# One low half in four by an adding DMA: a split float32 weight stream in a GLA and retention trunk

## The chip, the cores and the metric

The kernel runs on one core of a Trainium2 chip. The metric is device time in microseconds (us) from the start to the end of the program. Engines are named as in the profile: PE is TensorE (matrix products), PEld its weight loads, DVE is VectorE, ACT is ScalarE, POOL is GpSimd, SP is SyncE, which here only issues DMAs. "SPq" and "POOLq" are the DMA issues on the queues of SP and POOL.

## The reference

Two layers on 256 tokens of width 2048, in float32: a gated linear attention layer (GLA, 4 heads) and a retention layer (8 heads). Each normalises its input, projects it by a wide matrix to q, k, v and a gate, runs the attention in chunks of 64, normalises per head, multiplies by SiLU of the gate and projects back:

```python
proj = h @ w_in
q, k, v, gate = jnp.split(proj, [...], axis=-1)
...                                    # attention in chunks, per head
return (o * jax.nn.silu(gate)) @ w_out
```

The four weight matrices are almost all of the data that the program reads, and the products with them almost all of its arithmetic.

## The kernel before

The weights are laid out by the host as 60 groups; a group is 2048 x 512, that is 16 blocks of 128 x 512. A group is worked off in eight **sub-tiles** of two blocks each (`SUB = 2`), so there are 480 sub-tiles, in one fixed order from the first layer to the last. Each group is one product: q and k of a head (`group_w`, where the weights are the stationary operand), or v, the gate or a quarter of the output projection (`group_x`, where the activations are stationary).

TensorE multiplies here in a shorter float format (`F32R`). To keep float32 accuracy every operand is split in two: `hi` is the operand rounded to that format, and `lo` is the rest, operand minus `hi`. A product is then three matmuls, x_hi by w_hi, x_hi by w_lo, x_lo by w_hi (`mm3`, lines 184 to 186; lines 216 to 220 in `group_w`). The splits of the activations (`xhl`, `ogt`) are kept; those of the weights are made on the way:

- SP loads raw weights in tiles of 1 MB, two sub-tiles each, into three buffers (`emit_raw`, line 118), two tiles ahead (`DMA_LOOK`).
- ACT writes `hi` of a sub-tile as a rounding copy (line 151), DVE writes `lo` as raw minus hi (line 152). Each is 128 partitions by 1024 elements. There are three `hi` and three `lo` buffers.
- PE runs the 12 (`group_x`) or 16 (`group_w`) matmuls of the sub-tile.

`next_weights` is called once for each sub-tile, before its matmuls, and first emits all splits up to `LOOK = 2` ahead. So sub-tile i+2 takes the buffer that sub-tile i-1 used, and ACT can begin on it when PE has finished with i-1. The last group's eight splits go into memory that is free by then (`split_tiles`).

All other work (evacuating PSUM at the end of a group, the decays and scores of GLA, the rotary products, normalisation, transposes) is emitted between the sub-tiles in small steps (`side`, `advance`). The order on each engine is not that of the program text: a scheduler with its own timeline orders the instructions of each engine before the program is built, and each engine then runs its own list in order. POOL has little to do: eight loads each of `dm`, `gg` and `gb` and four of `fn` for the retention heads and the final norm, one of the positions, and 56 small additions in the GLA scores (line 568).

Of the kernel before, what the change touches and what calls it, by code (L numbers as in the profile page):

```python
# [10 lines left out]
F32 = mybir.dt.float32  # L11
F32R = mybir.dt.float32r
BF16 = mybir.dt.bfloat16
I32 = mybir.dt.int32
AF = mybir.ActivationFunctionType
ALU = mybir.AluOpType

P = 128
# [4 lines left out]
GW = 512  # L23
SUB = 2
NSUB = NKT // SUB
CHUNK = 4
LOOK = 2
DMA_LOOK = 2
GLA_H, RET_H, HK = 4, 8, 256
LEVELS = [1, 2, 4, 8, 16, 32, 64]  # L30
SCALE = 1.0 / 16.0
# [24 lines left out]
def kernel(  # L56
# [17 lines left out]
    nc = tc.nc  # L74
    pool = lambda name, bufs, **kw: ctx.enter_context(tc.tile_pool(name=name, bufs=bufs, **kw))
    one = pool("one", 1)
    raw_p = pool("raw", 3)
    hi_p = pool("hi", 3)
    lo_p = pool("lo", 3)
    v_p = pool("v", 2)  # L80
    o_p = pool("o", 2)
    sg_p = pool("sg", 2)
# [21 lines left out]
    last0 = (n_groups - 1) * NSUB  # L104

    def emit_raw(parts=1):
        c = emitted["raw"]
        if c >= n_groups * raws_per_group:
            return
        t = raw_p.tile([P, CHUNK, GW], F32, tag="raw", name=f"raw{c}")  # L110
        g, j = divmod(c, raws_per_group)
        src = w_all[g, :, j * CHUNK * GW : (j + 1) * CHUNK * GW].rearrange("p (k n) -> p k n", n=GW)
        step = CHUNK // parts
        raws[c] = t
        emitted["raw"] += 1

        def load(k):
            nc.sync.dma_start(t[:, k * step : (k + 1) * step, :], src[:, k * step : (k + 1) * step, :])

        if parts > 1:  # L120
            return load
        load(0)

    def split_tiles(i):
        if i < last0:
            hi = hi_p.tile([P, SUB, GW], F32R, tag="hi", name=f"hi{i}")
            lo = lo_p.tile([P, SUB, GW], F32R, tag="lo", name=f"lo{i}")
            return hi, lo
        j = i - last0
        hi = xhl[:, j * SUB : (j + 1) * SUB].rearrange("p k a t -> p k (a t)")  # L130
        if j < 4:
            if j % 2 == 0:
                tails.append(v_p.tile([P, 2, SUB, GW], F32R, tag="v", name=f"tail{j}"))
            return hi, tails[-1][:, j % 2]
        return hi, t4_p.tile([P, SUB, GW], F32R, tag="t4", name=f"tail{j}")
# [3 lines left out]
    def emit_split(pieces=1):  # L139
        i = emitted["sub"]  # L140
        if i >= n_groups * NSUB:
            return
        c, j = divmod(i, per_raw)
        while emitted["raw"] <= min(c + DMA_LOOK, n_groups * raws_per_group - 1):
            emit_raw()
        src = raws[c][:, j * SUB : (j + 1) * SUB, :]
        hi, lo = split_tiles(i)
        step = SUB // pieces
        for k in range(pieces):
            sl = slice(k * step, (k + 1) * step)  # L150
            nc.scalar.activation(hi[:, sl], src[:, sl], AF.Copy)  # L151
            nc.vector.tensor_tensor(lo[:, sl], src[:, sl], hi[:, sl].bitcast(F32), ALU.subtract)  # L152
        splits[i] = (hi, lo)
        if j == per_raw - 1:
            del raws[c]
        emitted["sub"] += 1
# [17 lines left out]
    def next_weights():  # L174
        i = state["sub"]
        while emitted["sub"] <= min(i + LOOK, n_groups * NSUB - 1):
            emit_split()
        state["sub"] += 1
        return splits.pop(i)
# [131 lines left out]
    emit_raw()  # L311
    make_xhl(0)
    emit_split(2)
    make_xhl(1)
    wa1 = t4_p.tile([P, NKT, 48], F32R, tag="lc", name="wa1", bufs=1)
# [676 lines left out]
```

## Time and profile before

| | |
|---|---|
| median of two runs | 1444.03 us (1443.39 to 1444.67) |
| span of the profiled execution, first to last instruction | 1441.2 us |
| PE busy | 1429.9 us |
| DVE, ACT, POOL busy | 910.3, 690.0, 44.1 us |
| granted TensorE clock | 0.999 |
| read from HBM | 263.49 MB |

The profile gives one execution. Its own time is its span, 1441.2 us; the median of the runs is 2.8 us above that, since a run's time also holds what lies before the first and after the last instruction. A group of instructions is shown as line, engine, operation, output tile, input tiles, shapes and count, then the busy time in us and the mean duration in ns, then the idle time of that engine just before these instructions and what ended it. In the timeline the columns are start, duration, engine, line, and in brackets how long the engine had been idle and who released it. Matmuls are pipelined, so that their durations overlap; their spacing is read from the starts.

### The profile page before, as it was taken

The numbers are of one execution on the slowest core, as the hardware profiler recorded it, in microseconds if no ns is written. First come the engines' busy times: TensorE is split into PE (matmuls) and PEld (weight loads), VectorE is DVE, ScalarE is ACT, GpSimd is POOL, SyncE is SP. The second block draws the span as 40 slices with busy tenths as digits, with TensorE's granted clock in tenths as the row PEclk, the third lists the DMA queues.
The fourth block names the chain that finished last, engine by engine and source line by source line (L and its number), as shares of the span: only waits on it lengthen the run. The fifth ranks groups of instructions, "written<-read, shape, count | busy, mean of one in ns | idle before, by whom it ended". The sixth has DMA issues, their size and how long they took to land.

```text
span 1441.2 us, 17504 instructions
## 1 busy us (share of the span) xinstructions
PE 1429.9 (99%) x6800; PEld 1181.0 (82%) x6800; DVE 910.3 (63%) x1430; ACT 690.0 (48%) x889; POOL 44.1 (3%) x98
## 2 busy tenths in 40 slices
PE   9999999999999999999999999999999999999997
PEld 6788888888888888888888888888888888888887
DVE  7595785545845764655666666664546666666654
ACT  4665654533554645454444444444344444444443
POOL 0010010000000010000000000000000000000000
PEclk9999999999999999999999999999999999999999
DMA  8643554555545555555555555555555555554562
GB/s 288 250 170 135 206 178 154 189 184 182 177 170 177 183 183 176 175 175 180 192 187 191 188 183 195 178 193 178 197 180 181 194 179 199 176 204 170 202 207 93
DMA packets 40499, 266.72 MB, mean 185 GB/s; under 512 B 4880, under 2 KB 5392, under 8 KB 9696
## 3 DMA queue, kind: packets, MB, share of 16 engines
q1 hardware_dynamic: 37536, 257.57, 51.2%
q0 software_dynamic: 2160, 6.95, 1.4%
q8 instruction: 53, 0.87, 0.2%
q10 hardware_dynamic: 720, 1.09, 0.2%
q14 instruction: 30, 0.25, 0.0%
HBM read 263.49 MB, written 2.10 MB: 184 GB/s over the span
## 4 chain that ended last, share of the span: by engine, by line
PE 99%; DMA 0%; SPq 0%; DVE 0%; ACT 0%; issue 0%
PE rqk_ps L219 8%; PE gv_ps L184 4%; PE gg_ps L185 4%; PE rv_ps L186 4%; PE gg_ps L186 4%; PE rv_ps L185 4%; PE rg_ps L185 4%; PE gv_ps L186 4%; PE rg_ps L186 4%; PE gv_ps L185 4%; PE rv_ps L184 4%; PE gg_ps L184 4%; PE rg_ps L184 4%; PE rqk_ps L220 4%; PE gqk_ps L219 4%; PE ra_ps L186 2%
## 5 line engine op out<-in xcount | busy, mean ns | idle before, releaser
L152 DVE TENSOR_TENSOR lo<-raw,hi 128x1024 fp32r<-128x1024 f32 (+1 forms) x473 | 577.6, 1223 | 439.9 <-ACT hi L151 421.5
L151 ACT ACTIVATE hi<-raw 128x1024 fp32r<-128x1024 f32 (+1 forms) x473 | 499.4, 1057 | 640.0 <-PE rg_ps L186 77.9
L219 PE MATMUL rqk_ps<-xhl,hi 128*128 128x512 f32 x480 | 165.9, 394 | 0.0
L220 PE MATMUL rqk_ps<-xhl,lo 128*128 128x256 f32 x480 | 127.2, 281 | 0.0
L219 PEld LDWEIGHTS rqk_ps<-xhl,hi 128*128 128x128 f32 x480 | 88.9, 188 | 16.1
L185 PE MATMUL gg_ps<-lo,xhl 128*128 128x512 f32 x256 | 102.1, 399 | 0.0
L185 PE MATMUL rv_ps<-lo,xhl 128*128 128x512 f32 x256 | 102.0, 399 | 0.0
L185 PE MATMUL gv_ps<-lo,xhl 128*128 128x512 f32 x256 | 102.0, 398 | 0.0
L186 PE MATMUL gv_ps<-hi,xhl 128*128 128x512 f32 x256 | 101.9, 398 | 0.0
L186 PE MATMUL gg_ps<-hi,xhl 128*128 128x512 f32 x256 | 101.7, 397 | 0.0
L186 PE MATMUL rv_ps<-hi,xhl 128*128 128x512 f32 x256 | 101.4, 396 | 0.0
L186 PE MATMUL rg_ps<-hi,xhl 128*128 128x512 f32 x256 | 101.3, 396 | 0.0
L185 PE MATMUL rg_ps<-lo,xhl 128*128 128x512 f32 x256 | 101.3, 396 | 0.0
L184 PE MATMUL gv_ps<-hi,xhl 128*128 128x512 f32 x256 | 94.7, 397 | 0.0
L184 PE MATMUL rv_ps<-hi,xhl 128*128 128x512 f32 x256 | 93.5, 396 | 0.0
L184 PE MATMUL rg_ps<-hi,xhl 128*128 128x512 f32 x256 | 93.5, 396 | 0.0
L184 PE MATMUL gg_ps<-hi,xhl 128*128 128x512 f32 x256 | 93.3, 397 | 0.0
L220 PEld LDWEIGHTS rqk_ps<-xhl,lo 128*128 128x128 f32 x480 | 89.2, 189 | 3.5
L219 PE MATMUL gqk_ps<-xhl,hi 128*128 128x512 f32 x240 | 80.0, 402 | 0.6 <-ACT hi L151 0.6
L220 PE MATMUL gqk_ps<-xhl,lo 128*128 128x256 f32 x240 | 57.6, 282 | 0.8 <-DVE lo L152 0.8
L186 PEld LDWEIGHTS rg_ps<-hi,xhl 128*128 128x128 f32 x256 | 48.1, 188 | 11.6
L185 PEld LDWEIGHTS rg_ps<-lo,xhl 128*128 128x128 f32 x256 | 48.1, 188 | 11.5
(265 smaller groups left out, 2395.2 us busy)
## 6 DMA issues: line engine op xcount, KB each, us to landing
raw<-in_w_all SPq DMA_DIRECT2D x238, 1024.0 KB, 4.8
resid<-in_x_n SPq DMA_DIRECT2D x2, 1024.0 KB, 7.8
gg<-in_gn_g POOLq DMA_DIRECT2D x8, 256.0 KB, 3.6
gb<-in_gn_b POOLq DMA_DIRECT2D x8, 256.0 KB, 4.5
dm<-in_dmat POOLq DMA_DIRECT2D x8, 192.0 KB, 2.6
raw<-in_w_all SPq DMA_DIRECT2D x4, 256.0 KB, 4.4
raw<-in_w_all SPq DMA_DIRECT2D x2, 512.0 KB, 7.3
xt<-in_x_t SPq DMA_DIRECT2D x2, 512.0 KB, 9.1
```

The lines of the kernel that those rows point to most:

```text
L151: nc.scalar.activation(hi[:, sl], src[:, sl], AF.Copy)
L152: nc.vector.tensor_tensor(lo[:, sl], src[:, sl], hi[:, sl].bitcast(F32), ALU.subtract)
L184: mm(ps, xh, hi[:, q, :], start=kt == 0, stop=False)
L185: mm(ps, xh, lo[:, q, :], start=False, stop=False)
L186: mm(ps, xl, hi[:, q, :], start=False, stop=kt == NKT - 1)
L219: mm(ps[c], wh, rhs[:, kt, :, :], start=kt == 0, stop=False)
L220: mm(ps[c][:, 0, :], wl, rhs[:, kt, 0, :], start=False, stop=False)
```

## The change

For the sub-tiles 11, 15, 19, ... 471 (from number 8 on, and outside the last group, each fourth one) `lo` is made in another way. ACT writes `hi` as before, then writes minus `hi` into a tile of a new pool with two buffers; then a DMA issued from POOL's queue reads the raw weights of the sub-tile a second time from HBM, 512 KB, and adds them onto that tile in SBUF. DVE has no part in these sub-tiles. In the other sub-tiles nothing changes.

Beside it `LOOK` goes from 2 to 3 and the `hi` pool from three to four buffers. The memory that the program sets aside for the descriptors of POOL's DMAs is set to 4096 bytes.

```diff
-LOOK = 2
+LOOK = 3
+ADDED = 4
+FIRST_ADDED = 8
...
-    hi_p = pool("hi", 3)
+    hi_p = pool("hi", 4)
     lo_p = pool("lo", 3)
+    add_p = pool("add", 2)
...
             hi = hi_p.tile([P, SUB, GW], F32R, tag="hi", name=f"hi{i}")
-            lo = lo_p.tile([P, SUB, GW], F32R, tag="lo", name=f"lo{i}")
+            if FIRST_ADDED <= i and i % ADDED == ADDED - 1:
+                lo = add_p.tile([P, SUB, GW], F32R, tag="add", name=f"added{i}")
+            else:
+                lo = lo_p.tile([P, SUB, GW], F32R, tag="lo", name=f"lo{i}")
...
+        if FIRST_ADDED <= i < last0 and i % ADDED == ADDED - 1:
+            g, s = divmod(i, NSUB)
+            nc.scalar.activation(hi, src, AF.Copy)
+            nc.scalar.activation(lo, hi.bitcast(F32), AF.Copy, scale=-1.0)
+            nc.gpsimd.dma_start(
+                lo.rearrange("p k n -> p (k n)"),
+                w_all[g, :, s * SUB * GW : (s + 1) * SUB * GW],
+                accum_op=ALU.add,
+            )
+            pieces = 0
         for k in range(pieces):
             sl = slice(k * step, (k + 1) * step)
             nc.scalar.activation(hi[:, sl], src[:, sl], AF.Copy)
...
-    nc = bacc.Bacc("TRN2", target_bir_lowering=False, num_devices=1)
+    nc = bacc.Bacc("TRN2", target_bir_lowering=False, num_devices=1, dynamic_dma_scratch_size=4096)
```

## The prediction

> **What bounds the kernel now.** I read the page's busy times, its chain and its costliest groups first, then the timeline of one quiet stretch, engine by engine, then the DMA issues.
>
> ```profile
> span 1441.2 us, 17504 instructions
> PE 1429.9 (99%) x6800; PEld 1181.0 (82%) x6800; DVE 910.3 (63%) x1430; ACT 690.0 (48%) x889; POOL 44.1 (3%) x98
> PE 99%; DMA 0%; SPq 0%; DVE 0%; ACT 0%; issue 0%
> L152 DVE TENSOR_TENSOR lo<-raw,hi 128x1024 fp32r<-128x1024 f32 (+1 forms) x473 | 577.6, 1223 | 439.9 <-ACT hi L151 421.5
> L151 ACT ACTIVATE hi<-raw 128x1024 fp32r<-128x1024 f32 (+1 forms) x473 | 499.4, 1057 | 640.0 <-PE rg_ps L186 77.9
> ```
>
> TensorE works in 1429.9 of 1441.2 us and the chain that ended last is 99% PE. It is idle for 11.3 us in all. Both engines of the split wait: DVE for hi (421.5 us in all), ACT for PE to give a hi buffer back. So whatever is taken off DVE gains nothing by itself; the largest gain open to the change is the 11.3 us, 0.8%. What matters is whether the new lo still comes before PE asks for it. The room for that is read from a quiet stretch (start, duration, engine, line):
>
> ```profile
> 1023.21 1.23 DVE L152 TENSOR_TENSOR lo<-raw,hi 128x1024 fp32r<-128x1024 f32 x1 [1.57 <-ACT hi L151]
> 1024.72 0.63 PE L184 MATMUL ra_ps<-hi,ogt 128*128 128x512 f32 x2
> 1025.19 0.40 PE L185 MATMUL ra_ps<-lo,ogt 128*128 128x512 f32 x1
> 1024.92 1.06 ACT L151 ACTIVATE hi<-raw 128x1024 fp32r<-128x1024 f32 x1 [1.74 <-PE ra_ps L186]
> 1026.02 1.23 DVE L152 TENSOR_TENSOR lo<-raw,hi 128x1024 fp32r<-128x1024 f32 x1 [1.57 <-ACT hi L151]
> 1027.52 0.63 PE L184 MATMUL ra_ps<-hi,ogt 128*128 128x512 f32 x2
> ```
>
> PE begins a sub-tile every 2.80 us (1024.72, 1027.52) and first needs lo 0.47 us into it (1025.19), since the two L184 matmuls that use hi stand ahead. ACT begins hi 0.20 us after PE has left an older sub-tile; DVE begins lo 0.04 us after hi has ended (1025.98 to 1026.02) and ends at 1027.25. With splits two ahead, that lo is asked for at 1024.72 + 2 x 2.80 + 0.47 = 1030.79: 3.5 us to spare, so PE never waits.
>
> **The change part by part.** 60 groups hold 480 sub-tiles; of numbers 8 to 471, those with remainder 3 by 4 are changed: 11, 15, ... 471, that is 116, the fourth and the last of each group of eight.
>
> *Removed:* 116 subtractions x 1.223 us = 142 us of DVE. All of it lay beside PE's work: gain 0. *Added on ACT:* 116 writes of -hi, of the shape of L151, 116 x 1.06 = 123 us; ACT goes from 690 to 813 us (56%), still with idle time. Behind a -hi stand the next hi and the evacuations. The next hi has 3.5 us to spare and more with three ahead, an evacuation starts at most 1.06 us later and its PSUM bank is not asked for at once: 0 on the path; without that cover it would be 1.06 us each. *Three splits ahead, four hi buffers:* the room grows by one sub-tile, 2.80 us. The three lo buffers serve as before, since one sub-tile in four uses the new pool. In the first eight, where none does, lo of sub-tile i+3 waits for PE to finish i, with 2.80 us x 3 still ahead of its use. Start-up work is re-ordered by it: between -3 and +3 us, bounded by the start-up's own idle time (40.00 - 36.72 below); I take 0.
>
> ```profile
> 0.00:40.00 40.00, 36.72 (x172) 28.27 (x173) 27.76 (x54) 17.36 (x24) 3.36 (x13) 1.00 0.85 301
> 40.00:360.00 320.00, 320.00 (x1483) 262.40 (x1482) 211.80 (x382) 172.89 (x230) 13.54 (x30) 1.00 0.52 180
> ```
>
> *The adding DMA* is the term that decides. Its room: from the moment PE leaves sub-tile i-4, three sub-tiles and 0.47 us pass until lo of i is asked for: 3 x 2.80 + 0.47 = 8.87 us. From it go ACT's start 0.20, hi 1.06, the hand-over 0.04, -hi 1.06, the hand-over to POOL 0.04: 2.40. That leaves **6.47 us from issue to landing**. For the fourth sub-tile of a group the split now falls on the group's start, where ACT empties PSUM first:
>
> ```profile
> 729.36 1.39 ACT L406 ACTIVATE rv<-rv_ps,r 128x512 fp32r<-128x512 f32 x2 [0.98 <-PE rv_ps L186]
> 730.65 1.05 ACT L151 ACTIVATE hi<-raw 128x1024 fp32r<-128x1024 f32 x1
> 729.86 0.63 PE L184 MATMUL rg_ps<-hi,xhl 128*128 128x512 f32 x2
> ```
>
> Here hi starts 0.79 us after PE's new group (729.86 to 730.65) in place of 0.20, which leaves **5.88 us**.
>
> What does the transfer need? No DMA of before adds, so it is bounded by the nearest rows (size, median us to landing):
>
> ```profile
> raw<-in_w_all SPq DMA_DIRECT2D x238, 1024.0 KB, 4.8
> gg<-in_gn_g POOLq DMA_DIRECT2D x8, 256.0 KB, 3.6
> gb<-in_gn_b POOLq DMA_DIRECT2D x8, 256.0 KB, 4.5
> dm<-in_dmat POOLq DMA_DIRECT2D x8, 192.0 KB, 2.6
> q1 hardware_dynamic: 37536, 257.57, 51.2%
> ```
>
> SP's queue moves 257.57 MB in 51.2% of 1441.2 us = 738 us, 349 GB/s while it works, so a 1 MB load (1.05 MB) is 3.0 us of engine time and 1.8 us around it. A POOL transfer of 192 KB has 0.56 us of engine time and 2.0 us around it. Lower bound of the adding one, 512 KB moved once and alone: 2.0 + 1.5 = 3.5 us. But an add needs the old contents of its destination as well as its source, so 1 MB passes: 2.0 + 3.0 = 5.0 us. Nor is it alone: the reader that frees the raw slot is now ACT's hi, so SP issues the next 1 MB load just as -hi begins, some 1.3 us (1.06 + 0.04 + about 0.2 for the shorter way of SP's queue) ahead of the add's own engine time. Of its 3.0 us some 1.7 are left to share the engines with, and the add, which arrives later, ends last: 5.0 + 1.7, less up to 0.4 where the two fill each other's start: 6.3 to 6.7; I take **6.5 us**.
>
> The Trainium skill (Collectives: The Full Stack, "The bandwidth ceiling: the fold count and why AG ≠ RS ≠ AR") says that an adding DMA has two source reads on the same read ring and so delivers half of a copy's rate. No run here shows it yet; by it the doubled figure is right, and by a plain copy the sum would be that of the first rival.
>
> On top comes what DVE does meanwhile:
>
> ```profile
> 743.57 0.54 POOL L835 DMA_DIRECT2D gb<-in_gn_b  x1 [21.20 <-DVE rm L854]
> 744.43 1.23 DVE L152 TENSOR_TENSOR lo<-raw,hi 128x1024 fp32r<-128x1024 f32 x1 [0.27 <-ACT hi L151]
> 750.46 0.54 POOL L834 DMA_DIRECT2D gg<-in_gn_g  x1 [6.35 <-DVE ro L858]
> 750.09 1.22 DVE L152 TENSOR_TENSOR lo<-raw,hi 128x1024 fp32r<-128x1024 f32 x1
> ```
>
> gb and gg are of one size; gb's issue is followed by a whole subtraction of DVE (744.43 to 745.66) and it lands after 4.5 us, gg's issue falls into the end of one and it lands after 3.6. So a subtraction just behind the issue is worth 0.9 us. An added sub-tile gives DVE no subtraction of its own, and the next comes after the 2.0 us around the issue, so only DVE's other work can do it: 910.3 - 577.6 = 333 us, 23% of the span. The same skill (SBUF — State Buffer, "Who interferes with whom") infers that a subtraction of two SBUF tiles does not stop descriptor writing; by it the 0.9 us would have another cause, and 116 x 0.33, some 34 us after the deduction below, would be all: 1478 us. The rows speak against it, so I keep it.
>
> **Sum.** At 6.5 us the last sub-tile of a group is 0.03 us late and the fourth 0.62: mean 0.33. In 23% of cases 0.9 us more: 0.93 and 1.52, mean 1.23. Weighted: 0.77 x 0.33 + 0.23 x 1.23 = 0.54 us. No two of the waits overlap (four sub-tiles lie between) and PE has nothing else to do: 116 x 0.54 = 62 us. The groups that start with L219 run four hi matmuls before a lo one; they are 12 of 60, and for them about half goes away: minus 6. So 1441.2 + 56 = 1497 us for the profiled execution; the median of the runs is 2.8 us above the span of before (1444.03), which gives 1500. I forecast **1498 us**.
>
> **The rivals.**
>
> *The add lands in time (not slower).* Place: the same DMA; the price falls to 0 once it lands within 5.9 us, and it stays inside 2% (29 us, 0.25 us for each of 116) up to about 6.1. For it: my 6.5 assumes that the add yields all of its overlap to the 1 MB load, and that both reads cost full pace; a POOL transfer of 192 KB lands after 2.6. Against it: the load's issue is freed at just that moment. Time: the same as before with three ahead, 1441 to 1447 us. Chance 0.41.
>
> *The add runs at a slower pace than copies.* Its arithmetic may not keep up with 349 GB/s. At half the pace, 3.0 us more: 3.03 and 3.62 late, 116 x 3.3 = 386 us, 1830 us. Nothing in the profile speaks for or against it. Chance 0.06; between it and my forecast all values are open.
>
> *POOL's queue blocks.* POOL runs in order. Its 28 parameter loads (dm, gg, gb, fn) and the 56 adds of the GLA heads wait for DVE or ACT:
>
> ```profile
> POOL dm L797 <- DVE rs L814: 536.7, 7, 195.1
> POOL gb L835 <- DVE rm L854: 148.5, 7, 21.2
> ```
>
> If one of these stands ahead of an adding DMA and its releaser comes later than that DMA is wanted, PE waits for it. Each such meeting costs at most about a sub-tile, 2.8 us: 28 x 2.8 = 78 us, 1520 us. For it: the long waits above. Against it: the order is made with the adds in it. Chance 0.05 as the main cause.
>
> *Faster by over 2%* would need 29 us where PE is idle 11.3 in all: 0.02.
>
> **How the numbers follow.** My forecast, a PE wait of some tenths of a us at most adds, has 0.46; its own range is 1473 (just over 2%) to 1586 (all adds 0.9 us later: 116 x 1.23 = 142 us). With the rival in time the range must start at 1440; it ends at 1600, leaving out the slow pace and a little on each side. About 2% is what a measurement of this kernel tells from no change. Slower: 0.46 + 0.06 + 0.05 = 0.57; within 2%: 0.41; faster: 0.02.
>
> **What would show it.** A row of PE waiting for DMA at L185 or L220, some 116 times, longer for the fourth sub-tile of a group than for the eighth; the adding DMA's time to landing about 6.5 us (under 5.9: the first rival; near 9.5: the second); DVE's busy time near 770 us, ACT's near 813; the 1 MB load's landing above 4.8; some 61 MB more read from HBM. If PE's idle time stays near 11 us I am wrong on the DMA; if PE waits with the add landing early, it was POOL's order.

## The result, and the profile after

| | before | after |
|---|---|---|
| median time | 1444.03 us | 1539.2 us (1538.24 to 1540.16, two runs) |
| span of the profiled execution | 1441.2 us | 1536.5 us |

The ratio is 1.0658 (95% interval 1.0641 to 1.0676): slower by 95 us. The page of the changed kernel, its busy times, chain and DMA issues (size, median us to landing):

```profile
span 1536.5 us, 17790 instructions
PE 1454.3 (95%) x6800; PEld 1186.2 (77%) x6800; DVE 775.3 (50%) x1314; ACT 802.5 (52%) x1005; POOL 147.9 (10%) x214
issue 48%; PE 33%; DMA 10%; ACT 4%; POOL 4%; DVE 1%; SPq 0%; POOLq 0%; ACTq 0%; DVEq 0%
L159 POOL DMA_DIRECT2D added<-in_w_all x116 | 100.6, 867 | 1214.2 <-ACT added L158 1012.6
raw<-in_w_all SPq DMA_DIRECT2D x238, 1024.0 KB, 5.0
added<-in_w_all POOLq DMA_DIRECT2D x116, 512.0 KB, 6.9
gg<-in_gn_g POOLq DMA_DIRECT2D x8, 256.0 KB, 6.9
gb<-in_gn_b POOLq DMA_DIRECT2D x8, 256.0 KB, 3.9
```

DVE has 135 us less to do and ACT 113 us more, and neither moved the end. PE's idle time went from 11.3 to 82.2 us (1536.5 - 1454.3), and its busy time grew by 24.4 us for the same 6800 matmuls. The chain, 99% PE before, now passes through the adding DMA. "issue" is time with no wait that the profile shows, and the rows below are surer than that share.

What one wait looks like, in the same stretch of work as the quiet one of the prediction (timeline of the changed kernel; L200 to L202 are the old L184 to L186):

```profile
1083.66 0.88 POOL L159 DMA_DIRECT2D added<-in_w_all  x1 [10.72 <-ACT added L158]
1088.95 0.63 PE L200 MATMUL ra_ps<-hi,ogt 128*128 128x512 f32 x2
1090.66 0.47 PE L201 MATMUL ra_ps<-added,ogt 128*128 128x512 f32 x1 [1.08 <-DMA added<-in_w_all]
```

PE runs the two hi matmuls that stand ahead and then waits for the add, issued 7.0 us earlier. I have measured each of the 116 places in the trace, as the start of the first matmul that uses the add, less the start of the one before and less the usual spacing. The fourth sub-tiles of the groups wait 1.33 us each, 77.2 us in all; the eighth wait 0.03 each, 1.7 us in all. So only one place in two waits: the fourth.

### The profile page after: what moved, and what is told of

Same layout as the page of the kernel before. It is cut to its first block, busy times and chain, and to the rows that moved or that the text cites. A ratio compares the mean times of both kernels' runs of the same rounds, so it can differ in the third digit from the quotient of the medians.

```text
span 1536.5 us, 17790 instructions
## 1 busy us (share of the span) xinstructions
PE 1454.3 (95%) x6800; PEld 1186.2 (77%) x6800; DVE 775.3 (50%) x1314; ACT 802.5 (52%) x1005; POOL 147.9 (10%) x214
## 3 DMA queue, kind: packets, MB, share of 16 engines
q0 software_dynamic: 18864, 67.77, 24.0%
## 4 chain that ended last, share of the span: by engine, by line
issue 48%; PE 33%; DMA 10%; ACT 4%; POOL 4%; DVE 1%; SPq 0%; POOLq 0%; ACTq 0%; DVEq 0%
DMA added<-in_w_all 9%; POOL added L159 3%; PE rv_ps L201 2%; PE rv_ps L202 2%; PE rv_ps L200 2%; PE gv_ps L201 2%; PE rg_ps L201 2%; PE gv_ps L202 2%; PE rg_ps L202 2%; PE gv_ps L200 2%; PE rg_ps L200 1%; ACT hi L157 1%; ACT added L158 1%; PE gg_ps L201 1%; PE rb_ps L201 1%
## 5 line engine op out<-in xcount | busy, mean ns | idle before, releaser
L168 DVE TENSOR_TENSOR lo<-raw,hi 128x1024 fp32r<-128x1024 f32 (+1 forms) x357 | 434.9, 1222 | 492.0 <-ACT hi L167 489.9
L167 ACT ACTIVATE hi<-raw 128x1024 fp32r<-128x1024 f32 (+1 forms) x357 | 375.9, 1056 | 350.0 <-PE rqk_ps L235 49.6
L157 ACT ACTIVATE hi<-raw 128x1024 fp32r<-128x1024 f32 x116 | 122.8, 1059 | 250.9 <-PE rv_ps L202 47.8
L159 POOL DMA_DIRECT2D added<-in_w_all x116 | 100.6, 867 | 1214.2 <-ACT added L158 1012.6
L158 ACT ACTIVATE added<-hi 128x1024 fp32r<-128x1024 f32 x116 | 122.8, 1059 | 2.8
L202 PE MATMUL gv_ps<-hi,xhl 128*128 128x512 f32 x256 | 103.3, 403 | 0.0
L236 PE MATMUL rqk_ps<-xhl,lo 128*128 128x256 f32 x384 | 102.5, 283 | 0.0
L202 PE MATMUL gg_ps<-hi,xhl 128*128 128x512 f32 x256 | 102.1, 399 | 0.0
L202 PE MATMUL rv_ps<-hi,xhl 128*128 128x512 f32 x256 | 101.7, 397 | 0.0
L202 PE MATMUL rg_ps<-hi,xhl 128*128 128x512 f32 x256 | 101.2, 395 | 0.0
L200 PE MATMUL gv_ps<-hi,xhl 128*128 128x512 f32 x256 | 99.8, 402 | 0.0
L200 PE MATMUL gg_ps<-hi,xhl 128*128 128x512 f32 x256 | 99.2, 401 | 0.0
L200 PE MATMUL rg_ps<-hi,xhl 128*128 128x512 f32 x256 | 98.6, 395 | 0.0
L200 PE MATMUL rv_ps<-hi,xhl 128*128 128x512 f32 x256 | 96.5, 397 | 0.0
L201 PE MATMUL gg_ps<-lo,xhl 128*128 128x512 f32 x192 | 76.4, 398 | 0.0
L201 PE MATMUL gv_ps<-lo,xhl 128*128 128x512 f32 x192 | 76.2, 397 | 0.0
L201 PE MATMUL rv_ps<-lo,xhl 128*128 128x512 f32 x192 | 76.0, 396 | 0.0
L201 PE MATMUL rg_ps<-lo,xhl 128*128 128x512 f32 x192 | 75.9, 396 | 0.0
L236 PEld LDWEIGHTS rqk_ps<-xhl,lo 128*128 128x128 f32 x384 | 73.0, 191 | 3.0
```

Of the source, the lines that this page charges most:

```text
L157: nc.scalar.activation(hi, src, AF.Copy)
L158: nc.scalar.activation(lo, hi.bitcast(F32), AF.Copy, scale=-1.0)
L159: nc.gpsimd.dma_start(lo.rearrange("p k n -> p (k n)"), w_all[g, :, s * SUB * GW : (s + 1) * SUB * GW], accum_op=ALU.add,)
L200: mm(ps, xh, hi[:, q, :], start=kt == 0, stop=False)
L201: mm(ps, xh, lo[:, q, :], start=False, stop=False)
L202: mm(ps, xl, hi[:, q, :], start=False, stop=kt == NKT - 1)
```

## The experiments

Nine kernels, all beside runs of the kernel before on the same chip. The lines are those of the changed kernel.

**Three ahead alone.** No adding DMA, four lo buffers in place of three and the pool of two:

```diff
-            if FIRST_ADDED <= i and i % ADDED == ADDED - 1:
+            if False:
...
-    lo_p = pool("lo", 3)
-    add_p = pool("add", 2)
+    lo_p = pool("lo", 4)
```

> Three splits ahead, four hi and four lo buffers and the smaller descriptor memory, but no adding DMA: every lo is subtracted on DVE. If the adds alone are what PE waits for: 1439 to 1447 us, as before, with PE's waits for lo as small as before. If the new order of the splits or the smaller descriptor memory costs by itself: above 1460 us.

1443.04 us, ratio 0.9997 (0.9987 to 1.0006). The order of the splits and the smaller descriptor memory together cost nothing and gain nothing.

**A copy in place of the add.**

```diff
-                accum_op=ALU.add,
```

> The DMA on POOL copies the raw weights over the tile in place of adding them; nothing else differs. lo is then the raw weight instead of raw minus hi, so the products are not those of the reference. Theory 1 (the landing time of an add, which has to move old contents and source, is the cause): half the bytes, so landing falls from 6.9 to about 5.2 us, the waits of the fourth sub-tiles fall from 1.3 to 0.2 to 0.4 us each, 1455 to 1470 us. Theory 2 (the order that the scheduler gave PE is the cause, whatever the landing): the fourth sub-tiles still wait about 1 us each, above 1510 us. If the contention with the 1 MB load sets the landing and not the doubled bytes: landing stays near 6.5 us, 1520 us.

1458.0 us, ratio 1.0098 (1.0078 to 1.0118). Busy times and the DMA's row:

```profile
PE 1433.7 (98%) x6800; PEld 1178.1 (81%) x6800; DVE 774.5 (53%) x1314; ACT 802.6 (55%) x1005; POOL 107.5 (7%) x214
L159 POOL DMA_DIRECT2D added<-in_w_all x116 | 62.0, 535 | 1159.7 <-ACT added L158 953.3
added<-in_w_all POOLq DMA_DIRECT2D x116, 512.0 KB, 5.1
```

1.8 us less to landing, and the waits of the fourth sub-tiles fall from 1.33 to 0.23 us, with everything else in place. So the larger part of the loss is what an add takes beyond a copy. Two rows say what that is. POOL is busy with the issue for 0.87 us in place of 0.53 (0.867 and 0.535 in the rows of L159), and POOL's DMA queue is busy for a larger share of the time (kernel before, changed kernel, copy):

```profile
q0 software_dynamic: 2160, 6.95, 1.4%
q0 software_dynamic: 18864, 67.77, 24.0%
q0 software_dynamic: 18864, 67.77, 13.9%
```

Multiplied by the spans (1441.2, 1536.5 and 1456.1 us), with the share of the kernel before taken off and divided by 116, that is 3.0 us of the DMA engines for an add and 1.6 for a copy. The profile counts the same 67.77 MB in both runs, so that the second read of an add shows in the time alone.

**The eighth sub-tiles alone, and the fourth alone.** The condition is changed in both places where it stands; the second kernel has `i % 8 == 3`:

```diff
-i % ADDED == ADDED - 1
+i % 8 == 7
```

> Adds only in the eighth sub-tile of each group (15, 23, ...), 58 of them or one more or less. By the room that I had worked out for all (6.47 us, less 0.25 for the slower hand-over to POOL, against 6.9 us of landing) each waits some 0.6 us: 1476 us. Theory 2 (the scheduler moves these lo matmuls behind matmuls of the next group, so that they have room and do not wait; what they do is hold the hi buffer that the next group's fourth sub-tile needs): no waits, 1441 to 1452 us.

> Adds only in the fourth sub-tile of each group (11, 19, ...), 59 or so. If the fourth is late by itself (ACT empties PSUM first, and then the add takes 6.6 us): waits as in the changed kernel, 1.3 us each, 1518 us. Theory 2 (it is late because the eighth of the group before keeps its hi buffer): hi starts 0.2 to 0.8 us after the group's start, the room from issue grows from 5.6 to about 6.3 us, the wait falls to 0.3 to 0.6 us each, 1460 to 1478 us.

1452.24 us (ratio 1.0058, 1.0038 to 1.0078) and 1474.65 us (1.0213, 1.0193 to 1.0234). First the eighth, then the fourth:

```profile
PE 1432.0 (99%) x6800; PEld 1180.0 (81%) x6800; DVE 843.2 (58%) x1372; ACT 753.2 (52%) x947; POOL 95.3 (7%) x156
added<-in_w_all POOLq DMA_DIRECT2D x58, 512.0 KB, 7.5
```

```profile
PE 1439.0 (98%) x6800; PEld 1180.5 (80%) x6800; DVE 838.8 (57%) x1372; ACT 751.0 (51%) x947; POOL 97.3 (7%) x156
added<-in_w_all POOLq DMA_DIRECT2D x58, 512.0 KB, 6.8
```

The adds of the eighth land late, after 7.5 us, and still nearly never make PE wait (7.1 us in all), because they have 9.4 us between issue and need. The fourth alone wait 0.44 us each, 25 us in all. The two costs, 9 and 31 us, add up to 40, not to 95, and the waits, 7 and 25 us, not to 79: with both in the kernel the one makes the other worse. This is the place where it does, on the timeline of the changed kernel at the end of a q and k group (PE's rows, then ACT's and POOL's, then PE's):

```profile
1151.56 1.09 PE L235 MATMUL rqk_ps<-xhl,hi 128*128 128x512 f32 x4
1152.49 0.40 PE L200 MATMUL rv_ps<-hi,xhl 128*128 128x512 f32 x1
1156.22 0.28 PE L236 MATMUL rqk_ps<-xhl,added 128*128 128x256 f32 x1
1157.85 0.40 PE L233 MATMUL rqk_ps<-xhl,hi 128*128 128x512 f32 x1
```

```profile
1155.49 1.06 ACT L157 ACTIVATE hi<-raw 128x1024 fp32r<-128x1024 f32 x1 [2.78 <-PE rv_ps L202]
1156.58 1.06 ACT L158 ACTIVATE added<-hi 128x1024 fp32r<-128x1024 f32 x1
```

```profile
1157.93 0.87 POOL L159 DMA_DIRECT2D added<-in_w_all  x1 [11.35 <-ACT rqk_h L246]
```

```profile
1162.75 0.63 PE L200 MATMUL rv_ps<-hi,xhl 128*128 128x512 f32 x2
1164.66 0.47 PE L201 MATMUL rv_ps<-added,xhl 128*128 128x512 f32 x1 [1.28 <-DMA added<-in_w_all]
```

The eighth sub-tile of `rqk` starts at 1151.56 with its hi matmuls. Its lo matmuls (L236 on `added`) were put by the scheduler into the middle of the next group, `rv`, at 1156.22, behind more than a whole sub-tile of it. So the eighth gets its room; but it keeps its hi buffer until 1157.85. The hi of the fourth sub-tile of `rv`, which by my count would take that buffer at 1152.5, is released by `rv` L202 instead: by the first sub-tile of its own group. It starts at 1155.49, its add is issued at 1157.93, and it is wanted at 1163.2.

Over the whole trace the hi of the fourth starts 3.15 us after the first matmul of its group in the mean when the eighth adds too, and 0.62 us when it does not. With the eighth, this hi waited for a matmul of its own group in 28 of the 58 groups; without, in none. In 18 others it stood on ACT's list right behind the evacuation of the group before, which comes late for the same reason: the last matmuls of that group do. So the moved matmuls delay the fourth in two ways, by the buffer and by the evacuation. The room from issue is 5.58 us in the mean when the eighth adds too, and 6.73 us when it does not; the landing is 6.64 and 6.82. That is the difference.

**Other places in the group.** The second and sixth sub-tile (still the second half of a raw tile), then the third and seventh (the first half, `i % 4 == 2`):

```diff
-i % ADDED == ADDED - 1
+i % 4 == 1
```

> The adds move to the second and the sixth sub-tile of each group (remainder 1 by 4): still the second half of a raw tile, so that the same load of 1 MB is freed with them, but away from the group's end. My count of the room (6.47 us, less 0.25 for POOL's hand-over) against a landing of 6.9 us gives some 0.7 us for each of 116: 1510 to 1530 us, both places alike. If the group's end alone made the waits: no place waits, 1441 to 1455 us.

> The adds move to the third and the seventh sub-tile (remainder 2 by 4): the first half of a raw tile, whose slot is not freed by them. The load of 1 MB that shared the DMA engines then starts some 2.8 us earlier and is over when the add begins. If that load is what lengthens the add: landing falls from 6.9 to 5.0 to 5.5 us, under the room of 6.2, and the time is 1441 to 1455 us. If the add takes 6.9 us by itself: waits of 0.7 us as in the run beside it, 1510 us and more.

1508.45 us (ratio 1.0448, 1.0425 to 1.0471) and 1466.53 us (1.0157, 1.0137 to 1.0178). The DMA's row of the first kernel, then of the second:

```profile
added<-in_w_all POOLq DMA_DIRECT2D x116, 512.0 KB, 6.8
```

```profile
added<-in_w_all POOLq DMA_DIRECT2D x116, 512.0 KB, 5.6
```

In the second and sixth place both wait alike, 0.51 and 0.42 us each, 54 us in all, so the waits need no group's end; the time came out just under the range expected. In the third and seventh place the landing falls to 5.6 us: the load of 1 MB is issued some 3 us ahead of the add in place of 1.36 (medians), and shares less of the engines with it. The time was expected under 1455 us and came out at 1466.5, a miss: about a dozen adds wait over 0.4 us, three of them 3 to 4 us. The trace shows most of these beside a late load: twelve adds had a load of SP still under way 4 us after their issue, landed after 7.8 us in the mean where the other 104 took 5.7, and hold 16 of the 20 us of waits.

**A copy in the third and seventh place.** Both edits together.

> Third and seventh sub-tiles as in the run before, and a copy in place of the add, so the products are not those of the reference: half the bytes and no load of 1 MB beside them. The four runs then give what each costs: add with the load 6.9, copy with the load 5.1, add without 5.6. If both costs are engine time that is shared, the copy without the load lands at 3.8 to 4.2 us; if the doubled bytes cost only where the engines are shared, at 5.1. Under the room in any case: 1441 to 1450 us.

1448.02 us, ratio 1.0027 (1.0015 to 1.0038).

```profile
added<-in_w_all POOLq DMA_DIRECT2D x116, 512.0 KB, 4.0
```

| us to landing | with the 1 MB load close ahead | with the load 1.6 us earlier |
|---|---|---|
| add | 6.9 | 5.6 |
| copy | 5.1 | 4.0 |

An add costs 1.6 to 1.8 us more than a copy of the same 512 KB, the load close ahead 1.1 to 1.3 us; the two costs add up. The DMA engines' time, worked out as for the first copy, is 3.2 us for the add with the load earlier and 1.9 for the copy there (27.0% and 16.5% of spans of 1466.1 and 1446.2 us). No run has the add or the copy without loads of SP beside it.

**Two ahead, with the adds.**

```diff
-LOOK = 3
+LOOK = 2
-    hi_p = pool("hi", 4)
+    hi_p = pool("hi", 3)
```

> The changed kernel with splits two ahead and three hi buffers, the adds as they are. The room shrinks by a sub-tile, 2.80 us. Taken from each add's room and landing in the changed kernel: the fourth sub-tiles wait 1.3 + 2.8 = 4.1 us, the eighth, with 8.9 us of room against 6.9, some 0.9 us: 58 x 5.0 = 290 us, about 1735 us. If the three splits ahead were not what gave the room: near 1539 us.

1788.96 us, ratio 1.239 (1.2327 to 1.2454). One sub-tile less of room costs 250 us more. The estimate was 54 us short: the waits came to 3.46 and 0.58 us (235 us by this count), and the longer ones brought PE's clock down. The trace has 48 stretches at half clock between its start and its end, 218 us in all; half of that is the 109 us that bring 235 near the 345 us above the kernel before.

```profile
core 0: 1779.4 us, clock 0.937
```

**More room.** Minus hi is written straight from the raw weights, and it and its DMA are emitted with the split of the sub-tile before:

```diff
-            nc.scalar.activation(lo, hi.bitcast(F32), AF.Copy, scale=-1.0)
-            nc.gpsimd.dma_start(...)
...
+        k = i + 1
+        if FIRST_ADDED <= k < last0 and k % ADDED == ADDED - 1:
+            g, s = divmod(k, NSUB)
+            early[k] = add_p.tile([P, SUB, GW], F32R, tag="add", name=f"added{k}")
+            nc.scalar.activation(early[k], raws[c][:, SUB : 2 * SUB, :], AF.Copy, scale=-1.0)
+            nc.gpsimd.dma_start(
+                early[k].rearrange("p k n -> p (k n)"),
+                w_all[g, :, s * SUB * GW : (s + 1) * SUB * GW],
+                accum_op=ALU.add,
+            )
```

> The same 116 adds, but minus hi is written straight from the raw weights (rounding is symmetric, so it is the same number), without waiting for hi's buffer, and it and its DMA are emitted one sub-tile earlier. The room from issue to landing grows by 2.8 us or more, above any landing seen (10.0 us at most, 6.9 at the median, against about 8.4 of room and more). If PE waits only because the room is short: the waits go and the time is 1441 to 1452 us. If the extra traffic, ACT's extra writes or POOL's order cost by themselves: above 1460 us.

1443.39 us, ratio 0.9996 (0.9986 to 1.0005).

```profile
span 1442.3 us, 17759 instructions
PE 1429.9 (99%) x6800; PEld 1181.0 (82%) x6800; DVE 773.3 (54%) x1314; ACT 803.6 (56%) x1005; POOL 147.5 (10%) x214
added<-in_w_all POOLq DMA_DIRECT2D x116, 512.0 KB, 6.0
```

All 116 adds, all of ACT's writes and all the second reads of the weights are there, and PE is as busy as before. The adds are issued 17.5 us before they are wanted in the mean, where it was 7.2 us in the changed kernel. That is 10 us more, where one sub-tile would be 2.8, and it is above the longest landing, 11.4 us. How much of it the earlier place gives, and how much comes of not waiting for a hi buffer, was not separated. This settles the cause: the work is free, the lateness is not. It also shows that the idea has nothing to gain here: DVE has 137 us less to do than before, and the time is the same.

## Why the prediction was right, and where it was not

The direction was right and the time lay in the range, which at 1440 to 1600 us was wide enough to hold no change as well. The sum was too small, 56 us against 95, and its parts were further off than that: 48 us for the fourth sub-tiles (77 measured), 14 for the eighth (2), 6 taken off for the q and k groups (nothing), and no term for the some 16 us by which matmuls stood wider apart. That the errors of the first two parts partly cancel is luck.

*The bound.* Right: taking 142 us from DVE gave nothing, in the kernel with more room as in the changed one. ACT's extra writes cost nothing either.

*The transfer.* Near in size and in its parts: 6.5 us forecast, 6.9 measured at the median (means 6.64 for the fourth, 6.94 for the eighth). The part for the doubled bytes was 1.5 us; an add took 1.6 to 1.8 us more than a copy, but 0.33 of these are POOL's longer issue, for which there was no term, and 1.4 the DMA engines' time. The part for the load was 1.7 less 0.4, measured 1.1 to 1.3; the rest, a copy, 3.5, measured 4.0. The Trainium skill (Collectives: The Full Stack, "The bandwidth ceiling: the fold count and why AG ≠ RS ≠ AR") gives the two source reads of an add for the reducing step of a collective. The adding DMA here agrees with it: 3.0 us of engine time against 1.6 for a copy.

*The room.* This step failed: "That leaves 6.47 us from issue to landing" for the eighth and 5.88 for the fourth, each for itself. It took PE's order as it stood. The scheduler moved the lo matmuls of the eighth in most groups past the group's end: 8.85 us of room, nearly no waits. The price was paid by the fourth of the next group, whose hi came late: 5.58 us, and 1.33 us of waiting in place of 0.62 to 1.52, weighted 0.83. Two smaller errors lie in the same step: POOL's hand-over took 0.29 us at the median in place of 0.04, and ACT put other work between hi and minus hi, 0.33 us in the mean for the fourth. Not waits that are independent of each other, then, but one set of places that pays for both.

*DVE's other work.* The term of 0.9 us in 23% of cases was wrong. In the changed kernel 88 adds have a subtraction of DVE within 0.8 to 2.6 us after the issue, and not only its other work as I had reckoned; they land after 6.83 us in the mean, the 28 without one after 6.67. The Trainium skill's inference (SBUF — State Buffer, "Who interferes with whom"), that a subtraction of two SBUF tiles does not hold up descriptor writing, fits these adds better than my reading of two rows. What sets gg and gb apart stands in the traces, and it is again the load of SP. Before, seven of the eight gb were issued 1.15 us after a 1 MB load and landed after 4.4 to 4.7 us; the eighth had none ahead and landed after 3.6. Six gg came 1.98 us after one and landed after 3.5 to 3.7; the other two came 1.2 to 1.3 us after one, and landed after 4.3 to 4.5 like gb. In the changed kernel gg lands after 6.9 us and gb after 3.9 (medians); there seven of the eight gg are issued while an add is under way, and one of the gb. So the 0.9 us goes with a load close ahead, whose price the sum already held.

*The groups with four hi matmuls ahead.* I took 6 us off for them. The adds of `rqk` wait 0.99 us in the mean, more than most, not less: that deduction has nothing behind it.

*PE's clock.* I had no term for it. Between its start and its end the trace has eight stretches of 3.4 or 6.8 us at half clock, each behind a wait of over 2 us (timeline of one, then the busy times of three stretches; the number before the last two is the granted clock):

```profile
1136.06 1.09 PE L235 MATMUL rqk_ps<-xhl,hi 128*128 128x512 f32 x4
1139.73 1.10 PE L236 MATMUL rqk_ps<-xhl,added 128*128 128x256 f32 x4 [2.58 <-DMA added<-in_w_all]
1140.63 0.63 PE L235 MATMUL rqk_ps<-xhl,hi 128*128 128x512 f32 x1
1141.06 0.41 PE L236 MATMUL rqk_ps<-xhl,added 128*128 128x256 f32 x1
```

```profile
1130.00:1139.80 9.80, 7.21 (x41) 5.99 (x39) 3.92 (x4) 4.86 (x5) 0.87 (x1) 1.00 0.74 175
1139.90:1143.20 3.30, 3.30 (x13) 2.92 (x13) 0.00 (x0) 0.00 (x0) 0.00 (x0) 0.50 0.65 273
1143.30:1150.00 6.70, 6.70 (x40) 5.92 (x39) 1.26 (x2) 4.22 (x4) 0.87 (x1) 1.00 0.69 186
```

After the wait that ends at 1139.73 an hi matmul takes 0.43 us to the next (1140.63 to 1141.06) in place of 0.23. The stretches begin on a grid of 3.413 us: those at 47.56, 74.87 and 102.17 lie eight steps apart. What counts is how much of a wait falls into one step. The changed kernel and the experiments have 62 such stretches between their starts and ends (8 here, 48 with two ahead, 6 in the others), and each began right after a step that held at least 2.07 us of waiting for adds; no step with up to 2.05 us was followed by one. Of the twelve waits of over 2 us here, the four that brought no stretch had 1.5 to 2.05 us in any one step.

The matmuls that do not use an add lost some 10 us more to wider spacing than in the kernel before, and these stand in PE's busy time. With some 85 us before and between the matmuls on the adds (79 before the first ones, and slow spacing behind) that makes the 95 us.

*The rivals.* "The add lands in time" did not happen as the change stands, and did in the kernel with more room, at the time that this rival gave (1441 to 1447; 1443.39 measured). "A slower pace than copies" is out: its 3.0 us of engine time are what the prediction worked out for a load of 1 MB, so at twice the bytes an add is no slower. "POOL's queue blocks" is out: an add was issued 0.29 us after minus hi at the median, and 0.59 us at the most.

## What to carry to other kernels

Where one engine is busy 99% of the time, moving work off another can gain next to nothing; what counts is by how much each result comes before it is wanted, and here a DMA in place of an engine's operation turned 1.2 us into 6.9. Count that room at each place of the loop, from the moment at which the buffer comes free, and expect a scheduler to move work, which can hold another buffer longer and delay what stands behind it. If such a result must come from a DMA, cut what its start waits for (here the hi buffer) before adding buffers: a start some 10 us earlier took the loss away, without any more memory.

## What the runs showed of the hardware

An adding DMA of 512 KB from POOL's queue landed after 6.9 us with a 1 MB load issued 1.4 us ahead, and after 5.6 with the load some 3 us ahead; a copy after 5.1 and 4.0. Its issue took POOL 0.87 us in place of 0.54 for the loads of before and 0.53 for a copy, and the DMA engines 3.0 us in place of 1.6 for a copy. At least 2.07 us of waiting within one step of a grid of 3.413 us halved TensorE's clock from the next step on, for 3.4 us or twice that; 2.05 us did not. The Trainium skill (TensorE: Matmul & The Clock Gate, "Part 1: The HAM clock gate (the "warmup" mystery)") has the halving after at least one idle window of about 3.4 us; the steps here are of that length, but 2.07 us of waiting in one brought it, so the idle time needed here was shorter than a window.
